# First tokens' pool means taken without the shift and earlier, their row sums later, and two pieces of the scale multiplied on TensorE

## The chip, the cores and the metric

The kernel runs on one core of a Trainium2 chip. The metric is the device time of one execution in microseconds (us); of several runs the median is given.

## The reference

One decoder block over 1024 tokens of width 1024, in float32. A conditioning vector `c` gives six vectors (shift, scale and gate of two halves). What matters here is the first half of the block:

```python
mod = jax.nn.silu(c) @ w_ada + b_ada
shift1, scale1, gate1, shift2, scale2, gate2 = ...
h = rms_norm(x, norm1_pre) * (1.0 + scale1) + shift1
z = h @ w_in                      # 1536 columns: u (512), v (512), pool (512)
y_a = spatial_gating(z[..., : 2 * D_A], ...)
y_b = multiscale_pool(z[..., 2 * D_A:], w_pool, b_pool, pool_scale)
mix = jnp.concatenate([y_a, y_b], axis=-1) @ w_out
x = x + gate1 * rms_norm(mix, norm1_post)
```

The pooling takes, in four groups of 128 channels, the mean over the last 2, 4, 8 or 16 tokens (over fewer at the beginning), subtracts the token itself and multiplies by a 128 by 128 matrix. The second half (a squared-ReLU MLP) is not touched.

## The kernel before

The 1024 tokens are worked in two halves of 512. `start` (L1340 onward) holds the whole first half up to the mixer's output projection, in an order written out by hand for all engines; what follows it up to the MLP (`project` and so on) is put in order by the framework, which may also set some of that work between instructions of `start`. Matrix products are done in three passes of two-part numbers (high part by high part, low by high, high by low), so each weight tile needs a copy on ACT (the high part) and a subtraction on DVE (the low part).

**The scale and the shift.** The rows of `w_ada` for scale 1 come in five pieces (`PIECES`: 128, 128, 256, 256, 256 columns), those for shift 1 in four pieces of 256 columns. `piece_sum` adds the eight rows of a piece on DVE, weighted by `silu_c`, into two running sums (even and odd rows; L1312 and L1314), and `both` (L1318) adds the two. `piece_end` (L1327) multiplies every 128 columns by a column of ones on TensorE, which sums over the partitions, and `ada_vector` (L188, L191) adds bias and gain on DVE. The first two scale pieces are what the first products wait for: `scaled_hi` (L1333, ACT) and `scaled_lo` (L1337, DVE) scale the transposed tokens, and `pool_pass` (L1421) multiplies them with the pool's columns of `w_in`.

**The shift by row sums.** In the first half the tokens are not shifted. The shift's part of `z` is one vector, the weights' rows weighted by the shift and summed. `row_sum` (L1524, L1526) makes that sum on DVE for the pool's columns (`bacc`, from the tiles `braw`), the value columns (`vacc`) and the gate columns (`uacc`), eight steps each; `row_vector` (L1531) sums over the partitions on TensorE. For the pool the vector is added to the four `zbs` by ACT (L1634), and only then `windowed` takes the means (L384 to L399 on DVE): it saves the last 16 tokens in `halo` for the second half, adds the tile to itself shifted one, two or three or four times, corrects the first tokens and subtracts the token.

**The order around it.** After the pool passes come the value products (a loop over four weight tiles, with the shift's pieces on DVE), then the gate passes `gate_pass(0)` to `gate_pass(7)` (L1596), the spatial products (L468), the pool's output (`pool_out`, L417 on TensorE, L419 and L421 on ACT, L422 on DVE), the first weight tiles of the projection (`stream.fill`), and `spatial_end` (L473, L478, then the split at L91 and L94). `load_x(1)` loads the second half's tokens into the four tiles that `braw` lay in, so it waits for the row sums of the pool. `measure` (L308) and `apply` (L317) normalise them.

`project` then multiplies with `w_out` in two passes over columns (L85 to L87, tile `po`); the order of the operands is pool pairs 0 and 1, 2 and 3, then spatial 0 and 1, 2 and 3. Between the two passes it calls `prepare`, which transposes the second half's tokens (L324) and scales them (L329).

```python
MIX_ORDER = (2, 3, 0, 1)
...
            token_pass(ym, MIX_ORDER, f"po{h}_{dh}", done)
            if dh == 0:
                between()
```

Of the kernel before, what the change touches and what calls it, by code (L numbers as in the profile page):

```python
# [8 lines left out]
F32 = mybir.dt.float32  # L9
# [3 lines left out]
ALU = mybir.AluOpType  # L13
# [27 lines left out]
def block_kernel(  # L41
# [1264 lines left out]
    def piece_sum(blk, c0, n, ts):  # L1306

        def step(kt):
            def run():
                acc = acc_of[blk][kt % 2][:, c0:c0 + n]  # L1310
                if kt < 2:
                    nc.vector.tensor_scalar(acc, ts[kt], silu_c[:, kt:kt + 1], None, ALU.mult)  # L1312
                else:
                    nc.vector.scalar_tensor_tensor(acc, ts[kt], silu_c[:, kt:kt + 1], acc, ALU.mult, ALU.add)  # L1314
            return run
        def both():
            a, b = [acc_of[blk][o][:, c0:c0 + n] for o in range(2)]
            nc.vector.tensor_tensor(a, a, b, ALU.add)  # L1318

        return [step(kt) for kt in range(KT)] + [both]  # L1320

    def piece_end(blk, c0, n, split=False):
        pa = ps_tile(f"pa{blk}_{c0}")
        nk = n // P
        for k in range(nk):
            at = c0 + k * P
            nc.tensor.matmul(pa[:, k:k + 1], lhsT=acc_of[blk][0][:, at:at + P], rhs=ones[:, 0:1], start=True, stop=True)  # L1327
        rest = lambda: ada_vector(blk, pa[:, 0:nk], range(c0 // P, c0 // P + nk))
        return rest if split else rest()

# [8 lines left out]
    def start():  # L1339
# [50 lines left out]

        g = piece_sum(1, *PIECES[0], sc[0])
        first(0)
# [9 lines left out]
        third(2)  # L1402
        weave(g)
        second(3)
        scale_rest = piece_end(1, *PIECES[0], split=True)
        third(3)
# [7 lines left out]
        hT = []  # L1414
        pbs = [ps_tile(f"pb0_{j}") for j in range(NG)]

# [16 lines left out]
        hT.append(scaled_hi(pts[0], 0))  # L1433
        g = piece_sum(1, *PIECES[1], sc[1])
        weave(g[:KT // 2])
        scaled_lo(hT[0], pts[0], 0)
        weave(g[KT // 2:])
        pool_lo(0)
        pool_pass(0, 0)
        pool_pass(0, 1)  # L1440
        piece_end(1, *PIECES[1])
        his(1)
        pool_pass(0, 2)
        more(3)
        g = piece_sum(1, *PIECES[2], sc[2])
        weave(g[:KT // 2])
# [58 lines left out]
        value_lo(0, 0)  # L1505
        value_lo(0, 1)
        pool_pass(KT - 1, 1)
        pool_pass(KT - 1, 2)
# [10 lines left out]

        bacc, vacc, uacc = rows_of("b"), rows_of("v"), accp.tile([P, 512], F32, tag="junk", bufs=1, name="shift_wu")  # L1520

# [30 lines left out]
        for kp in range(NQ):  # L1552
            if kp == 0:
                sh.append(piece(0, 2 * QC, QC))
                value_tiles(1)
                value_hi(1)
                gate_load(0)
# [24 lines left out]
            if kp == 1:  # L1582
                rest_b()
                turn()
            if kp == 2:
                offsets()


# [24 lines left out]
        for i in range(NT):  # L1613
            nc.tensor.matmul(pvs[i], lhsT=ones_r, rhs=vb[:, 0], start=False, stop=False)
            nc.tensor.matmul(pvs[i], lhsT=ones_r, rhs=vb[:, 1], start=False, stop=True)
        weave(sums_b(0, 4), sums_u(0, 2))
        gate_load(3)
        gate_pass(2)
        gate_pass(3)
        steps, vs = values(0, pvs)  # L1620
        weave(steps[:4], sums_b(4, 8))
        gate_hi(2)
        gate_lo(2, 0)
        gate_lo(2, 1)
        gate_pass(4)
        weave(steps[4:], sums_u(2, 6))
        gate_hi(3)
        gate_lo(3, 0)
        gate_lo(3, 1)
        gate_pass(5)  # L1630
        bvec = row_vector(bacc, "b")
        for j in range(NG):
            z = zbs[j][:, HALO:]
            nc.scalar.activation(z, z, AF.Identity, bias=bvec[:, j:j + 1])  # L1634
        weave(sums_u(6, 8), windowed(0, 0, zbs[0]))
        gate_pass(6)
# [24 lines left out]
        return ya + [y for y, low in yb]  # L1661


    with tc.manual_schedule(engines={E.DVE, E.Activation, E.PE, E.Pool, E.SP}):
# [45 lines left out]
```

## Time and profile before

| what | value |
|---|---|
| runs | 923.02, 923.35, 924.67 us (median 923.35) |
| profiled execution | 922.04 us, span 920.3 us |
| busy | PE 889.4 us (97%), DVE 687.4 (75%), ACT 419.1 (46%), POOL 89.1 (10%) |
| granted TensorE clock, mean | 0.995 |

Times in the rows are us from the start of the span. PE is TensorE's matmuls, PEld its weight loads, DVE VectorE, ACT ScalarE, POOL GpSimd, SPq the queue from which SyncE issues DMAs. A busy PE in a window is not PE at its peak, since the ends of matmuls are modelled and the next one starts before the last has ended; so the rate of TensorE is better read from the starts of its instructions.

### The profile page before, as it was taken

What the parts mean: (1) busy time and instruction counts of PE and PEld (TensorE: products, weight loads), DVE (VectorE), ACT (ScalarE), POOL (GpSimd) and SP (SyncE); (2) the same over time, 40 slices, a digit from 0 to 9 for tenths busy, and PEclk for the clock granted to TensorE, in tenths of its full rate; (3) what the DMA queues carried; (4) which work ended last, traced back from release to release, by engine and by line L of the source; (5) the groups of instructions that cost most, each with busy time, mean ns of one, the idle gap of its engine ahead of it and who ended that gap; (6) DMA issues with size and microseconds to landing.
All of it is one profiled execution on the core that took longest, in us unless ns stands there. A gap on an engine that the chain in (4) does not pass through costs nothing.

```text
span 920.3 us, 10782 instructions
## 1 busy us (share of the span) xinstructions
PE 889.4 (97%) x3960; PEld 722.9 (79%) x3960; DVE 687.4 (75%) x980; ACT 419.1 (46%) x558; POOL 89.1 (10%) x147
## 2 busy tenths in 40 slices
PE   5999999999999989999999999999999999999995
PEld 3788678888887768888888888778888888888883
DVE  6989888799759896766666657567887774569796
ACT  3323674334367474444444354544455433434331
POOL 4001020013003001111100101100000000000032
PEclk9999999999999999999999999999999999999998
DMA  9934256575734148543444434499975884334664
GB/s 316 357 113 143 91 161 188 178 252 183 234 87 149 54 129 274 185 138 130 168 150 158 139 136 155 160 320 389 338 242 198 294 279 117 109 110 145 207 212 154
DMA packets 114105, 173.52 MB, mean 189 GB/s; under 512 B 6098, under 2 KB 61442, under 8 KB 114052
## 3 DMA queue, kind: packets, MB, share of 16 engines
q1 hardware_dynamic: 104292, 135.03, 45.8%
q0 software_dynamic: 9760, 37.80, 10.8%
q8 instruction: 31, 0.51, 0.2%
q14 instruction: 22, 0.18, 0.1%
HBM read 135.06 MB, written 37.75 MB: 188 GB/s over the span
## 4 chain that ended last, share of the span: by engine, by line
PE 53%; issue 32%; DVE 8%; ACT 4%; DMA 2%; POOL 1%; SPq 0%; POOLq 0%; DVEq 0%; ACTq 0%
PE a L828 6%; PE a L829 6%; PE a L830 6%; PE p L830 3%; PE p L829 3%; PE p L828 3%; PE pb L1421 3%; PE po L85 2%; PE pu L1596 2%; PE po L86 2%; PE po L87 2%; PE pv L85 2%; PE pv L87 2%; PE pv L86 2%; PE b L828 1%
## 5 line engine op out<-in xcount | busy, mean ns | idle before, releaser
L85 PE MATMUL m<-thi,shi 128*128 128x512 f32 x448 | 174.3, 389 | 0.0
L86 PE MATMUL m<-tlo,shi 128*128 128x512 f32 x448 | 174.3, 389 | 0.0
L87 PE MATMUL m<-thi,slo 128*128 128x512 f32 x448 | 174.3, 389 | 0.0
L94 DVE TENSOR_TENSOR slo<-s,shi 128x1024 fp32r<-128x1024 f32 x56 | 68.4, 1222 | 55.8 <-ACT shi L91 55.8
L91 ACT CAST shi<-s 128x1024 fp32r<-128x1024 f32 x56 | 58.9, 1052 | 106.2 <-PE m L86 64.1
L86 PEld LDWEIGHTS m<-tlo,shi 128*128 128x128 f32 x448 | 84.1, 188 | 17.6
L87 PEld LDWEIGHTS m<-thi,slo 128*128 128x128 f32 x448 | 84.1, 188 | 17.5
L85 PEld LDWEIGHTS m<-thi,shi 128*128 128x128 f32 x448 | 84.1, 188 | 17.3
L91 ACT CAST thi<-wt 128x1024 fp32r<-128x1024 f32 x40 | 42.1, 1052 | 39.7 <-DVE wt L571 31.3
L91 ACT CAST whi<-w_raw 128x1024 fp32r<-128x1024 f32 x28 | 29.3, 1053 | 52.0 <-DMA w_raw<-in_w_in_dram 15.4
L571 DVE TENSOR_TENSOR wt<-wt,b 128x1024 f32<-128x1024 f32 x32 | 39.1, 1222 | 15.0 <-DMA b<-in_w_fc_dram 13.1
L94 DVE TENSOR_TENSOR tlo<-wt,thi 128x1024 fp32r<-128x1024 f32 x40 | 48.9, 1223 | 1.4
L571 DVE TENSOR_TENSOR S<-c,F 128x1024 f32<-128x1024 f32 x12 | 14.7, 1224 | 41.8 <-ACT F L860 41.8
L94 DVE TENSOR_TENSOR wlo<-w_raw,whi 128x1024 fp32r<-128x1024 f32 x28 | 34.1, 1220 | 7.0 <-ACT whi L91 7.0
L858 ACT COPY F<-a 128x512 f32<-128x512 f32 x16 | 9.4, 586 | 57.0 <-PE a L830 57.0
L291 POOL TENSOR_TENSOR f<-msf,neg_half 128x1 f32<-128x1 f32 x8 | 7.2, 901 | 282.5 <-DVE msf L1160 282.5
L603 DVE TENSOR_TENSOR lob<-wa,hib 128x1024 fp32r<-128x1024 f32 x16 | 19.6, 1225 | 16.4 <-ACT hib L598 16.4
L598 ACT CAST hic<-wo 128x1024 fp32r<-128x1024 f32 x16 | 16.8, 1051 | 31.3 <-DVE wo L571 31.3
L598 ACT CAST hib<-wa 128x1024 fp32r<-128x1024 f32 x16 | 16.8, 1050 | 30.3 <-DVE wa L571 30.3
L181 DVE SCALAR_TENSOR_TENSOR ada_acc<-ada_raw,silu_c,ada_acc 128x1024 f32<-128x1024 f32 x21 | 26.9, 1280 | 3.9 <-DMA ada_raw<-in_w_ada_dram 3.8
L85 PE MATMUL po<-whi,ybs 128*128 128x512 f32 x64 | 25.8, 406 | 1.6 <-ACT yb L419 0.9
L830 PE MATMUL p<-hS,loc 128*128 128x512 f32 x64 | 25.4, 397 | 1.9 <-DVE loc L603 1.9
(311 smaller groups left out, 2194.4 us busy)
## 6 DMA issues: line engine op xcount, KB each, us to landing
s<-fD SPq DMA_DIRECT2D x56, 512.0 KB, 4.1
wt<-in_w_fc_dram SPq DMA_DIRECT2D x40, 512.0 KB, 5.1
ada_raw<-in_w_ada_dram SPq DMA_DIRECT2D x24, 512.0 KB, 4.8
fD<-S POOLq DMA_DIRECT2D x16, 768.0 KB, 3.7
wa<-in_w_fc_dram SPq DMA_DIRECT2D x20, 512.0 KB, 4.2
piece<-in_w_ada_dram SPq DMA_DIRECT2D x16, 512.0 KB, 8.3
w_raw<-in_w_out_dram SPq DMA_DIRECT2D x16, 512.0 KB, 4.6
wo<-in_w_fc_dram SPq DMA_DIRECT2D x16, 512.0 KB, 4.6
```

Source lines behind the costliest of these rows:

```text
L85: nc.tensor.matmul(ps, lhsT=ah, rhs=bh, start=start, stop=False)
L86: nc.tensor.matmul(ps, lhsT=ah, rhs=bl, start=False, stop=False)
L87: nc.tensor.matmul(ps, lhsT=al, rhs=bh, start=False, stop=stop)
L91: nc.scalar.copy(hi, src)
L94: nc.vector.tensor_tensor(lo, src, hi.bitcast(F32), ALU.subtract)
L181: nc.vector.scalar_tensor_tensor(acc, t, silu_c[:, kt:kt + 1], acc, ALU.mult, ALU.add)
L571: nc.vector.tensor_tensor(o, a, b, op)
L598: nc.scalar.copy(unit_tiles(kind, n)[0], src)
L828: nc.tensor.matmul(ps, lhsT=ah, rhs=bh, start=first, stop=False, skip_group_check=not start)
L829: nc.tensor.matmul(ps, lhsT=ah, rhs=bl, start=False, stop=False, skip_group_check=not start)
L830: nc.tensor.matmul(ps, lhsT=al, rhs=bh, start=False, stop=last, skip_group_check=not start)
L1421: nc.tensor.matmul(pbs[j], lhsT=w[:, j * P:(j + 1) * P], rhs=a, start=k == 0 and n == 0, stop=k == KT - 1 and n == 2)
```

## The change

- The first two pieces of the scale (128 columns each) are no longer summed on DVE. `piece_direct` gives TensorE the eight rows of a piece as stationary operands, with a column of `silu_c` each, and adds them up in PSUM.
- The other seven pieces keep the two running sums on DVE, but `both` is gone: `piece_end` multiplies both sums by ones and adds them in PSUM.
- The pool's row sums are not added to `zbs`. A constant falls out of "mean minus token", so the means of the first half are taken without it, and only the `halo` that the second half reads gets it, in `shift_halo`, called between the two passes of the projection.
- So `windowed(0, 0)` and `(0, 1)` move into the loop of the value products, `(0, 2)` ahead of `gate_pass(2)`; the first three `pool_out` move ahead of `gate_pass(5)`; the first weight tile of the projection is split before `gate_pass(6)`.
- The eight row sums of `bacc` move behind the first two `spatial_end`, and `load_x(1)` and `measure` behind the last.
- The second weight tile of the value products is split before the last pool passes.

```diff
-        def both():
-            a, b = [acc_of[blk][o][:, c0:c0 + n] for o in range(2)]
-            nc.vector.tensor_tensor(a, a, b, ALU.add)
-
-        return [step(kt) for kt in range(KT)] + [both]
+        return [step(kt) for kt in range(KT)]
...
         for k in range(nk):
             at = c0 + k * P
-            nc.tensor.matmul(pa[:, k:k + 1], lhsT=acc_of[blk][0][:, at:at + P], rhs=ones[:, 0:1], start=True, stop=True)
+            for o in range(2):
+                nc.tensor.matmul(pa[:, k:k + 1], lhsT=acc_of[blk][o][:, at:at + P], rhs=ones[:, 0:1], start=o == 0, stop=o == 1)
...
+    def piece_direct(blk, c0, ts):
+        pa = ps_tile(f"pa{blk}_{c0}")
+        for kt in range(KT):
+            nc.tensor.matmul(pa[:, 0:1], lhsT=ts[kt], rhs=silu_c[:, kt:kt + 1], start=kt == 0, stop=kt == KT - 1)
+        return lambda: ada_vector(blk, pa[:, 0:1], range(c0 // P, c0 // P + 1))
...
-        weave(g)
+        scale_rest = piece_direct(1, 0, sc[0])
         second(3)
-        scale_rest = piece_end(1, *PIECES[0], split=True)
         third(3)
         scale_rest()
...
         pool_lo(0)
         pool_pass(0, 0)
+        piece_direct(1, P, sc[1])()
         pool_pass(0, 1)
-        piece_end(1, *PIECES[1])
         his(1)
...
         value_lo(0, 1)
+        value_tiles(1)
+        value_hi(1)
         pool_pass(KT - 1, 1)
...
             if kp == 1:
                 rest_b()
                 turn()
+                weave(windowed(0, 0, zbs[0]))
             if kp == 2:
                 offsets()
+                weave(windowed(0, 1, zbs[1]))
...
-        weave(sums_b(0, 4), sums_u(0, 2))
         gate_load(3)
+        weave(sums_u(0, 2), windowed(0, 2, zbs[2]))
         gate_pass(2)
         gate_pass(3)
         steps, vs = values(0, pvs)
-        weave(steps[:4], sums_b(4, 8))
+        weave(steps[:4])
...
-        weave(steps[4:], sums_u(2, 6))
+        weave(steps[4:], sums_u(2, 4))
...
+        yb = [pool_out(0, j, pair_of(diffs[0], j)) for j in range(3)]
         gate_pass(5)
-        bvec = row_vector(bacc, "b")
-        for j in range(NG):
-            z = zbs[j][:, HALO:]
-            nc.scalar.activation(z, z, AF.Identity, bias=bvec[:, j:j + 1])
-        weave(sums_u(6, 8), windowed(0, 0, zbs[0]))
+        weave(sums_u(4, 6))
+        stream.fill(1)
+        yb[0][1]()
+        yb[1][1]()
         gate_pass(6)
+        weave(sums_u(6, 8))
         gate_pass(7)
         psp = [spatial_products(0, j, vs) for j in range(2)]
         uvec = row_vector(uacc, "u")
         us = [gate(0, j, pus[j], uvec[:, j:j + 1]) for j in range(NHEAD)]
-        weave(windowed(0, 1, zbs[1]), windowed(0, 2, zbs[2]))
         psp += [spatial_products(0, j, vs) for j in range(2, NHEAD)]
-        yb = [pool_out(0, j, pair_of(diffs[0], j)) for j in range(2)]
         weave(windowed(0, 3, zbs[3]))
-        for y, low in yb:
-            low()
-        stream.fill(1)
-        yb += [pool_out(0, j, pair_of(diffs[0], j)) for j in range(2, NG)]
+        yb += [pool_out(0, 3, pair_of(diffs[0], 3))]
+        yb[2][1]()
+        stream.fill(2)
+        yb[3][1]()
+        bacc = accp.tile([P, 512], F32, tag="acc", name="shift_wb")
+        rest_u = sums_b(0, KT)
+        ya = []
+        for j in range(NHEAD):
+            ya.append(spatial_end(0, j, psp[j], us[j]))
+            if j == 1:
+                stream.fill(3)
+            weave(rest_u[4 * j:4 * j + 4])
         load_x(1)
         measure, apply = normalise(1, "a")
-        ya = []
-        for j in range(NHEAD):
-            if j in (1, 2):
-                stream.fill(1 + j)
-            ya.append(spatial_end(0, j, psp[j], us[j]))
-            if j < 2:
-                yb[2 + j][1]()
-            if j == 2:
-                measure()
+        measure()
         apply()
+
+        def shift_halo():
+            bvec = row_vector(bacc, "b")
+            for j in range(NG):
+                nc.vector.tensor_scalar(halo[:, j, :], halo[:, j, :], bvec[:, j:j + 1], None, ALU.add)
+
+        late["halo"] = shift_halo
...
     def prepare(key, h, n, name):
         def run():
+            late["halo"]()
             nxt[key] = hidden(h, n, name)
         return run
```

## Rows read from the trace of the kernel before

**Rows 1.** Windows: stretch, length, busy time (x instructions) of each engine, clock, DMA.

```profile
24.29:46.10 21.81, 21.81 (x107) 17.46 (x107) 20.17 (x48) 8.43 (x15) 0.86 (x5) 1.00 1.07 357
46.10:71.50 25.40, 25.40 (x121) 20.53 (x120) 21.66 (x53) 6.40 (x9) 0.00 (x0) 1.00 0.32 106
71.50:100.50 29.00, 29.00 (x153) 24.81 (x152) 27.31 (x57) 10.69 (x18) 4.14 (x4) 1.00 0.47 145
100.50:107.40 6.90, 5.06 (x13) 1.77 (x12) 6.15 (x10) 6.58 (x11) 0.00 (x0) 1.00 0.00 0
107.40:129.60 22.20, 22.05 (x93) 17.42 (x94) 17.60 (x26) 14.49 (x22) 5.30 (x8) 1.00 0.54 158
```

**Rows 2.** Timeline, 11 to 15 us: start, duration, engine, instruction.

```profile
11.15 0.90 PE L1389 MATMUL pta<-ident,x 128*128 128x128 f32 x3 [0.47 <-DVE x L1385]
13.44 0.58 PE L1327 MATMUL pa<-ones,ada_acc 128*128 128x1 f32 x2 [1.39 <-DVE ada_acc L1318]
14.62 0.69 ACT L1333 ACTIVATE ha<-pta,scale 128x512 fp32r<-128x512 f32 x1 [0.78 <-DVE ada_acc L1312]
```

**Rows 3.** Timeline, 18 to 24.3 us, around the second and third piece.

```profile
18.94 0.42 PE L1327 MATMUL pa<-ones,ada_acc 128*128 128x1 f32 x2
19.22 1.84 PE L1421 MATMUL pb<-ha,wblo 128*128 128x512 f32 x4
20.90 0.60 PE L324 MATMUL pta<-ident,x 128*128 128x128 f32 x4
...
23.34 0.42 DVE L1318 TENSOR_TENSOR ada_acc<-ada_acc,ada_acc 128x256 f32<-128x256 f32 x1
...
23.82 0.61 PE L1327 MATMUL pa<-ones,ada_acc 128*128 128x1 f32 x4 [1.39 <-DVE ada_acc L1318]
```

**Rows 4.** Chain that ended last, around the fourth piece's products: start, length, what.

```profile
30.97 0.34 PE pa L1327 x4
31.31 1.98 PE pb L1421 x8
```

**Rows 5.** Instructions on the sums of the pieces: the additions of both sums.

```profile
L1318 DVE TENSOR_TENSOR ada_acc<-ada_acc,ada_acc x9: 291/424/426, 13.1 to 66.1; 128x256 f32<-128x256 f32 x7, 128x128 f32<-128x128 f32 x2
```

**Rows 6.** Groups of DVE instructions, 92 to 104 us, one addition of the means.

```profile
L389 DVE TENSOR_TENSOR s<-zb 128x527 f32<-128x527 f32 x4 | 2.7, 702 | 0.0
```

**Rows 7.** Chain that ended last, 98 to 101 us.

```profile
98.02 0.79 PE pau L1531 x8
...
100.70 0.88 PE pp L417 x2
```

**Rows 8.** Instructions on zb, 85 to 105 us: ACT's additions of the shift.

```profile
L1634 ACT ACTIVATE zb<-zb,vecb x4: 707/708/723, 90.9 to 92.7; 128x512 f32<-128x512 f32 x4
```

**Rows 9.** Timeline, 104 to 108 us, TensorE's waits ahead of the projection.

```profile
104.26 1.04 ACT L91 CAST whi<-w_raw 128x1024 fp32r<-128x1024 f32 x1
...
107.42 0.50 PE L85 MATMUL po<-whi,ybs 128*128 128x512 f32 x1 [0.88 <-ACT yb L419]
```

**Rows 10.** Instructions on the pool's row sums and on weight splits: ns min/median/max.

```profile
L1526 DVE SCALAR_TENSOR_TENSOR shift_wb<-x,shift,shift_wb x7: 741/745/755, 75.2 to 83.7; 128x512 f32<-128x512 f32 x7
...
L94 DVE TENSOR_TENSOR wlo<-w_raw,whi x7: 1211/1219/1226, 105.3 to 125.9; 128x1024 fp32r<-128x1024 f32 x7
```

**Rows 11.** Timeline, 127 to 130 us, the last spatial end and the second half's tokens.

```profile
127.06 0.68 DVE L94 TENSOR_TENSOR yas<-ya,yas 128x512 fp32r<-128x512 f32 x1
127.66 2.73 DVE L317 TENSOR_SCALAR x<-x,r_a 128x1024 f32<-128x1024 f32 x4
...
129.61 3.65 PE L324 MATMUL pta<-ident,x 128*128 128x128 f32 x32
```

**Rows 12.** Instructions on the second half's token tiles, 70 to 135 us.

```profile
L109 SPq DMA_DIRECT2D x<-in_x_dram x4: 327/328/467, 77.1 to 84.5; - x4
L308 ACT ACTIVATE junka<-x x4: 1054/1057/1058, 119.7 to 123.3; 128x1024 bf16<-128x1024 f32 x4
...
DMA to landing us min/median/max: 4.2/5.0/5.7
```

More of the change, by code (lines that the diff above doesn't have):

```diff
@@ L1315, in step, with piece_end @@
             return run
-        def both():
-            a, b = [acc_of[blk][o][:, c0:c0 + n] for o in range(2)]
-            nc.vector.tensor_tensor(a, a, b, ALU.add)
-        return [step(kt) for kt in range(KT)] + [both]
-    def piece_end(blk, c0, n, split=False):
+        return [step(kt) for kt in range(KT)]
+    def piece_end(blk, c0, n):
         pa = ps_tile(f"pa{blk}_{c0}")
@@ L1326, in piece_end @@
             at = c0 + k * P
-            nc.tensor.matmul(pa[:, k:k + 1], lhsT=acc_of[blk][0][:, at:at + P], rhs=ones[:, 0:1], start=True, stop=True)
-        rest = lambda: ada_vector(blk, pa[:, 0:nk], range(c0 // P, c0 // P + nk))
-        return rest if split else rest()
+            for o in range(2):
+                nc.tensor.matmul(pa[:, k:k + 1], lhsT=acc_of[blk][o][:, at:at + P], rhs=ones[:, 0:1], start=o == 0, stop=o == 1)
+        ada_vector(blk, pa[:, 0:nk], range(c0 // P, c0 // P + nk))
+    def piece_direct(blk, c0, ts):
[3 more added lines that the diff above has]
+        return lambda: ada_vector(blk, pa[:, 0:1], range(c0 // P, c0 // P + 1))
     def scaled_hi(ps, k):
@@ L1389, in third @@
                 nc.tensor.transpose(out=pts[k][:, i * P:(i + 1) * P], in_=xs[i][:, k * P:(k + 1) * P], identity=ident)
-        g = piece_sum(1, *PIECES[0], sc[0])
+        pbs = [ps_tile(f"pb0_{j}") for j in range(NG)]
         first(0)
@@ L1414, in start @@
         hT = []
-        pbs = [ps_tile(f"pb0_{j}") for j in range(NG)]
         def pool_pass(k, n):
@@ L1433, in start @@
         hT.append(scaled_hi(pts[0], 0))
-        g = piece_sum(1, *PIECES[1], sc[1])
-        weave(g[:KT // 2])
+        g = piece_sum(1, *PIECES[2], sc[2])
         scaled_lo(hT[0], pts[0], 0)
-        weave(g[KT // 2:])
         pool_lo(0)
         pool_pass(0, 0)
+        piece_direct(1, P, sc[1])()
         pool_pass(0, 1)
-        piece_end(1, *PIECES[1])
         his(1)
@@ L1444, in start @@
         more(3)
-        g = piece_sum(1, *PIECES[2], sc[2])
         weave(g[:KT // 2])
@@ L1518, in rows_of @@
             return fact.tile([P, 512], F32, tag="f", name=f"shift_w{n}")
-        bacc, vacc, uacc = rows_of("b"), rows_of("v"), accp.tile([P, 512], F32, tag="junk", bufs=1, name="shift_wu")
+        vacc, uacc = rows_of("v"), accp.tile([P, 512], F32, tag="junk", bufs=1, name="shift_wu")
         def row_sum(acc, k, src):
@@ L1554, in start @@
                 sh.append(piece(0, 2 * QC, QC))
-                value_tiles(1)
-                value_hi(1)
                 gate_load(0)
@@ L1640, in start @@
         us = [gate(0, j, pus[j], uvec[:, j:j + 1]) for j in range(NHEAD)]
-        weave(windowed(0, 1, zbs[1]), windowed(0, 2, zbs[2]))
         psp += [spatial_products(0, j, vs) for j in range(2, NHEAD)]
-        yb = [pool_out(0, j, pair_of(diffs[0], j)) for j in range(2)]
         weave(windowed(0, 3, zbs[3]))
-        for y, low in yb:
-            low()
-        stream.fill(1)
-        yb += [pool_out(0, j, pair_of(diffs[0], j)) for j in range(2, NG)]
+        yb += [pool_out(0, 3, pair_of(diffs[0], 3))]
[10 more added lines that the diff above has]
+            weave(rest_u[4 * j:4 * j + 4])
         load_x(1)
         measure, apply = normalise(1, "a")
-        ya = []
-        for j in range(NHEAD):
-            if j in (1, 2):
-                stream.fill(1 + j)
-            ya.append(spatial_end(0, j, psp[j], us[j]))
-            if j < 2:
-                yb[2 + j][1]()
-            if j == 2:
-                measure()
-        apply()
+        measure()
+        apply()
+        def shift_halo():
[3 more added lines that the diff above has]
+        late["halo"] = shift_halo
         return ya + [y for y, low in yb]
+    late = {}
     with tc.manual_schedule(engines={E.DVE, E.Activation, E.PE, E.Pool, E.SP}):
```

## The prediction

> **What bounds the kernel now.** I read the windows first, then the chain, then the timelines of the two places where TensorE stands still. In the windows from 24.29 to 100.50 us TensorE's busy time equals the length of each stretch, while DVE has 1.6 to 3.7 us left in each [rows 1]; the chain runs through TensorE there, piece by piece without a gap [rows 4]. So each instruction added to TensorE in that stretch is paid in full, and each freed on DVE or ACT is worth something only through what it lets start earlier. Two places are open. At the start, up to 24 us, the products wait for the scale: TensorE waits 1.39 us for the first piece's sum and again 1.39 us for the third's [rows 2, 3]. And ahead of the projection, in 100.50 to 107.40 us, TensorE has 13 instructions only [rows 1]. From 107.42 us on the projection runs steadily [rows 9], and behind it TensorE stays the bound, since its busy share of the whole span is 97%; what is won or lost by 133 us should reach the end unchanged.
>
> **The start.** The first piece loses about 2.3 us of sums on DVE and gains eight products on TensorE, 16 instructions, since such a float32 product is two (two instructions for the one product of the second piece [rows 3]). Behind a full queue two of them take 0.28 us, 18.94 to 19.22 [rows 3], thus 0.14 each and 2.24 us a piece. The bounds are 0.085 (a quarter of the 0.34 of four at TensorE's other speed [rows 4]) and 0.29 (half of the 0.58 from a standstill [rows 2]). I take 0.14, because the eight follow each other and TensorE is as slow there. The transposes of the third tile end at about 11.9, so the products end at 14.1 and the scaling, 0.6 us behind the old ones' end at 14.02 [rows 2], starts at about 14.85 in place of 14.62. The second piece's products go behind the first pass (four matmuls, 1.75 us from 15.6), 17.35 to 19.6, against an end at 19.22 before [rows 3]: 0.4 us later. From there DVE's chain to the third piece's products is the same, less `both` (0.42 us [rows 3]), plus four products (0.34 us [rows 4]): a gain of 0.08. So the start is **+0.3 us**, with bounds of -1.6 (0.085 each, both pieces) and +3.0 (0.29 each, the second piece partly hidden). DVE's saved sums are worth nothing here: the wait moves from DVE to TensorE.
>
> **TensorE's clock.** The pool pass at 19.22 us takes 1.84 us for four matmuls, about 0.44 each, though the row grants 1.00; from 31.31 eight take 1.98, 0.25 each [rows 3, 4]. That is the lower level, 1.2 GHz, and then 2.4 GHz; it rose at about 20.9 us, where four transposes go in 0.35 us [rows 3], behind the first tile's pool passes. The Trainium skill (TensorE: Matmul & The Clock Gate, "What's actually happening") says that the slow state is the default and that activity releases it. By that rule the direct products, which fill the gap before 13.44, could bring the rise forward; it is a rival below, priced from the rows.
>
> **The other pieces.** Seven `piece_end` get four more instructions each; the third piece's are in the sum above, six remain: 6 x 0.34 = **+2.04 us** [rows 4], all on TensorE where nothing covers it. The lower bound is 0, if their weight loads hid under the matmuls in front; but the old four did not. A rule speaks against the change here: the Trainium skill (TensorE: Matmul & The Clock Gate, "LDWEIGHTS (loading the stationary operand)") puts a load at columns divided by 1.2 per ns, 107 ns for 128 columns. By it the six pieces would cost 2.6 us; the row's 0.085 us is shorter, and the row decides.
>
> **DVE in the loop of the value products.** Each `both` of 256 columns frees 0.42 us [rows 5]: four in this loop, 1.7. `windowed(0, 0)` and `(0, 1)` bring three additions and two subtractions of 0.70 [rows 6], 3.5 us, and four short ones on 16 columns; I count 4.2 us. From 21.66 of 25.40 us [rows 1] DVE goes to 24.2 of 26.8 (four pieces at 0.34 longer). I cost this at nothing: the cover is 2.6 us, and the shift's pieces are needed one weight tile later. The earlier copy of the second weight tile gives DVE another 2 us at the loop's beginning.
>
> **The pool's vector.** Its eight products, 0.79 us like the gate's [rows 7], leave the gate stage: **-0.79 us**. ACT's four additions of 0.71 [rows 8] leave too; ACT is half idle there [rows 1], so that is worth nothing by itself.
>
> **The idle time ahead of the projection.** From the spatial products' end at 100.70 [rows 7] to 107.42 [rows 9] are 6.72 us. In it lie eight pool products' instructions of 0.44 (0.88 for two [rows 7]), 3.5 us, and three matmuls of the projection, 0.7. So 2.57 us are idle. With three of the four pool products, the first weight tile and two operands ready earlier, the projection can start right behind the fourth: **-2.57 us**; the bound on the other side is 0.
>
> Up to there: 0.3 + 2.04 - 0.79 - 2.57 = -1.0 us.
>
> **The projection's first pass.** What is late next is DVE. In 107.40 to 129.60 us it has 4.6 us left [rows 1], and eight row sums come in: 8 x 0.745 = 6.0 us by duration [rows 10], about 5.3 by their starts. They stand between the spatial ends, ahead of the third weight tile's low part (1.22 us [rows 10]) and of the last two operands. Also the second weight tile's high part now stands on ACT behind the gates and the fourth pool output, where DVE waits for it, as ACT's copy stood at 104.26 before [rows 9]. The last operand was ready at 127.74 [rows 11] and TensorE's last matmuls just behind it, so it cannot come later without moving the pass's end. My count has DVE reach it between 127 and 129, so the pass ends at about 129.6 as before, and the 1.0 us that TensorE had won is lost again: **+1.0 us**, between 0 and +2. Then the pool's products come back, **+0.79 us**, between 0 (hidden in TensorE's wait) and 0.79.
>
> **Sum.** -1.0 + 1.0 + 0.8 = +0.8 us on 922.04 of the profiled execution, 922.8; the median of the runs lies 1.31 above that execution, so I forecast 924.2. A measurement of this kernel can tell about 0.2%, 1.85 us.
>
> **The rivals.**
> - *The second half's tokens are late (slower).* `load_x(1)` went out from 77.1 to 84.5 and was squared by 119.7 to 123.3, 1.2 us a tile [rows 12]. Now the last tile is free only after the row sums, at about 121.9; 4.2 to 5.0 us to landing [rows 12] make 126.5. ACT squares behind the last spatial end, four times 1.2 from about 126.4: 131.1; the power on POOL and the scaling bring 132.8. The transposes started at 129.61 [rows 11]; if they keep their place and wait for the last tile, they end 2.9 us later. It decides as soon as the tokens are scaled later than about 130.5 and the framework has set no products of the second pass in front. For it: the move behind all spatial ends. Against: the framework orders this part and may fill it. In place of the 0.8: 0.4 + 2.9 = +3.3, **926.7**.
> - *All of TensorE's win is kept*, because DVE's waits for ACT are filled with splits and the last operand comes in time: -1.0 + 0.8 = -0.2, **923.1**. For it: the splits of later tiles already stand between spatial ends. Against: 6.0 us into 4.6.
> - *The clock rises early*, at or before 17 us. The second piece's products take 0.085 and the passes 0.23 each, so the third piece comes 1.5 to 2 us sooner: **922.2**, or 921.2 with the rival before. Against: between 12 and 15 us the engine still stands.
> - *The clock stays low longer or the direct products cost 0.29*: +2.5 more, **926.7**.
> - *The change does not close the gap*: TensorE still waits for ACT ahead of the projection, as it did for 0.88 us on the pool output [rows 9], since the fourth output and the second tile stay late. Then the 2.57 stay: **926.8**.
>
> **How the numbers follow.** The forecast gets 0.40, late tokens 0.24, the kept win 0.12, the early clock 0.16, the late one 0.04, the open gap 0.04. Faster by over 0.2% (below 921.5) is most of the early clock and a part of the kept win: 0.18. Slower (above 925.2) is the late tokens, the two last cases and the edge of the forecast: 0.35. The rest, 0.47, is no change. The range reaches from the early clock with the kept win, 921.0, to late tokens with some of the start's upper bound, 927.4. The forecast's own is 922.8 to 925.4, from 0 to +2 in the pass and the start's smaller errors.
>
> **What would show it.** Right: 16 instructions on the first piece in about 2.2 us; eight in 0.68 for each later piece; no wait ahead of the projection; the row sums between spatial ends, and TensorE waiting there for a split or a spatial operand. Wrong: transposes that wait for the scaled tokens (the first rival), a matmul of 0.23 us before 19 us (the clock), a wait of the gate passes on DVE (my cover in the loop), or a first pass that ends before 129 us.

## The result and the profile after

The changed kernel takes 939.55 us (937.38 to 939.84, 4 runs), the kernel before 923.79 beside it (923.02 to 924.67): a ratio of 1.0165, with a 95% interval of [1.0147, 1.0184], 15.8 us slower. The forecast was 924.2, at most 927.4. The profiled execution is the fastest of the four (the others take 939.4 to 939.8): 937.38 us, its span 935.3; that is 15.0 us over the span before, and the difference is whole by the second pass of the projection: the transposes ahead of it end at 148.65 us where they ended at 133.26 [rows 11], 15.4 later.

**Where it builds up.** First TensorE's timeline at the start, which answers [rows 2, 3]. L1331 is a direct piece, L1324 the third piece's products, L1423 the pool's passes.

```profile
12.38 3.41 PE L1331 MATMUL pa<-silu_c,piece 128*128 128x1 f32 x16
...
18.89 3.41 PE L1331 MATMUL pa<-silu_c,piece 128*128 128x1 f32 x16
22.16 2.05 PE L1423 MATMUL pb<-ha,wbhi 128*128 128x512 f32 x4
24.01 1.91 PE L1423 MATMUL pb<-ha,wblo 128*128 128x512 f32 x4
...
26.43 1.46 PE L1423 MATMUL pb<-ha,wbhi 128*128 128x512 f32 x4
27.72 0.95 PE L1324 MATMUL pa<-ones,ada_acc 128*128 128x1 f32 x8
28.53 1.18 PE L1423 MATMUL pb<-ha,wbhi 128*128 128x512 f32 x4
```

The next work starts 3.27 us after a direct piece's first instruction: 0.20 us for each of the 16, not 0.14. And the passes at 22.16 and 24.01 take 0.43 to 0.46 us a matmul, the lower level of 1.2 GHz; only the pass at 26.43 gets faster. Before, that happened at 20.9 us [rows 3]. The third piece's products end at 28.53 instead of 24.29: **+4.2**. About half a us of that is the tokens' arrival, which differs between executions: the last transposes ahead of the first piece's products start at 11.69 us, where they started at 11.15 [rows 2].

The windows behind it, in the columns of [rows 1]: stretch, length, busy time of PE, PEld, DVE, ACT and POOL, granted clock.

```profile
28.53:78.14 49.61, 49.61 (x250) 40.86 (x250) 42.74 (x103) 14.37 (x22) 0.83 (x5) 1.00 0.54 181
78.14:109.30 31.16, 31.16 (x154) 25.30 (x152) 24.91 (x48) 13.87 (x21) 3.37 (x4) 1.00 0.29 86
109.30:143.48 34.18, 26.42 (x106) 19.70 (x104) 24.56 (x39) 16.56 (x27) 3.09 (x4) 0.94 0.59 184
143.48:148.65 5.17, 5.17 (x33) 5.17 (x34) 4.93 (x7) 4.34 (x12) 4.95 (x5) 0.71 0.19 32
```

From the third piece's products to the gate the kernel before needed 47.21 us, 24.29 to 71.50 [rows 1]; now it is 49.61, without idle time: **+2.4**, six pieces with four more instructions each, 0.40 a piece. A later piece in the chain, eight instructions where [rows 4] had four in 0.34:

```profile
35.25 0.78 PE pa L1324 x8
36.03 1.98 PE pb L1423 x8
```

Then comes what the change was for: TensorE is busy in all 31.16 us up to the projection.

```profile
108.84 1.02 PE L417 MATMUL pp<-diff,wpl 128*128 128x512 f32 x2
109.30 0.80 PE L85 MATMUL po<-whi,ybs 128*128 128x512 f32 x1
```

The projection begins right behind the last pool product, without the waits of [rows 9]. Counted by the steady pace of 0.23 us a matmul, it began before at 107.42 less the three matmuls already done, 106.7, and now at 109.7 (its second matmul starts at 109.93), 3.0 later. Start and pieces had put it 6.6 late: the gap and the pool's vector gave back **3.6**.

And the pass that follows loses that and much more: 33.8 us to the first transpose instead of 22.9, **+10.9**, and another 1.5 in the transposes. TensorE is busy for 26.42 of 34.18 us. Its waits there, us in total, times, longest:

```profile
PE pta L324 <- DVE x L317: 2.7, 1, 2.7
PE po L85 <- ACT yas L91: 2.0, 1, 2.0
PE po L85 <- ACT whi L91: 1.7, 1, 1.7
PE pab L1532 <- DVE shift_wb L1527: 1.1, 1, 1.1
```

They are 7.5 us. The rest is the pool vector's products, now here, and slow matmuls: behind the wait for the third spatial operand one starts only every 0.43 us, and the 32 transposes take 5.17 us in place of 3.65 [rows 11], at a granted clock of 0.71. An estimate of what the slow instructions add: seven matmuls from 133.19 take 3.1 us where 0.23 each make 1.6, and with the 1.5 of the transposes that is about 3 us.

```profile
133.19 0.80 PE L85 MATMUL po<-whi,yas 128*128 128x512 f32 x1 [2.05 <-ACT yas L91]
133.78 0.63 PE L86 MATMUL po<-wlo,yas 128*128 128x512 f32 x1
134.21 0.63 PE L85 MATMUL po<-whi,yas 128*128 128x512 f32 x1
...
143.48 5.17 PE L324 MATMUL pta<-ident,x 128*128 128x128 f32 x32 [2.71 <-DVE x L317]
```

The order in time is waits first, clock second: up to 130 us the row grants 1.00, though the wait for the third weight tile (1.72 us, ending at 122.77) and the one for the row sums (1.14) lie there, and only behind them it falls.

```profile
120.00:130.00 10.00, 7.17 (x29) 4.87 (x27) 9.03 (x12) 5.43 (x6) 0.00 (x0) 1.00 0.67 190
130.00:140.00 10.00, 7.78 (x30) 6.08 (x31) 7.55 (x15) 4.21 (x10) 0.95 (x1) 0.83 0.75 270
```

Who is late is read from the timelines of DVE and ACT: four row sums hold the second spatial end; the second operand's cast at 121.15 waits 4.91 us for it; and the third weight tile's cast, with which TensorE starts at 122.77, stands behind that cast.

```profile
116.88 0.48 DVE L1525 TENSOR_SCALAR shift_wb<-x,shift 128x512 f32<-128x512 f32 x1
117.40 2.33 DVE L1527 SCALAR_TENSOR_TENSOR shift_wb<-x,shift,shift_wb 128x512 f32<-128x512 f32 x3
...
137.48 0.75 DVE L179 TENSOR_SCALAR ada_acc<-ada_raw,silu_c 128x1024 f32<-128x1024 f32 x1 [2.24 <-DMA ada_raw<-in_w_ada_dram]
138.15 0.69 DVE L94 TENSOR_TENSOR yas<-ya,yas 128x512 fp32r<-128x512 f32 x1
...
142.69 2.73 DVE L317 TENSOR_SCALAR x<-x,r_a 128x1024 f32<-128x1024 f32 x4
```
```profile
121.15 0.62 ACT L91 CAST yas<-ya 128x512 fp32r<-128x512 f32 x1 [4.91 <-DVE ya L478]
121.67 3.90 ACT L91 CAST whi<-w_raw 128x1024 fp32r<-128x1024 f32 x4
```

Later DVE waits 2.24 us for a transfer of the gate vector's weights (L179), with the last operand's low part behind it in its queue; and the tokens, loaded from 118.2 to 130.1 instead of 77.1 to 84.5 [rows 12], are scaled at 142.69.

### The profile page after: what moved, and what is told of

Same layout as the page of the kernel before. It is cut to its first block, busy times and chain, and to the rows that moved or that the text cites. A ratio compares the mean times of both kernels' runs of the same rounds, so it can differ in the third digit from the quotient of the medians.

```text
span 935.3 us, 10873 instructions
## 1 busy us (share of the span) xinstructions
PE 900.9 (96%) x4016; PEld 735.5 (79%) x4016; DVE 681.3 (73%) x959; ACT 417.1 (45%) x554; POOL 90.3 (10%) x147
## 3 DMA queue, kind: packets, MB, share of 16 engines
q0 software_dynamic: 9760, 37.80, 10.5%
## 4 chain that ended last, share of the span: by engine, by line
PE 54%; issue 31%; DVE 8%; ACT 3%; DMA 2%; POOL 1%; SPq 0%; POOLq 0%; DVEq 0%; ACTq 0%
PE a L828 5%; PE a L829 5%; PE a L830 5%; PE pb L1423 3%; PE p L830 3%; PE p L829 3%; PE p L828 3%; PE po L87 2%; PE pu L1597 2%; PE po L85 2%; PE po L86 2%; PE pv L85 2%; PE pv L87 2%; PE pv L86 2%; PE b L828 1%
## 5 line engine op out<-in xcount | busy, mean ns | idle before, releaser
L85 PE MATMUL po<-whi,yas 128*128 128x512 f32 x64 | 25.8, 411 | 3.8 <-ACT yas L91 2.0
```

Of the source, the lines that this page charges most:

```text
L85: nc.tensor.matmul(ps, lhsT=ah, rhs=bh, start=start, stop=False)
```

## The experiments

All on the same kernel size, each beside runs of the kernel before (923.1 to 923.9 in the five sets; each difference is to its own set). **My theory after the result:** three independent losses, the one-column products on TensorE at the start, the doubled products of six pieces, and an order of the projection's first pass that makes DVE, ACT and the queues wait in turn. **The rivals:** the parts act on each other; or the low clock is the cause and the waits follow from it; or DVE simply has too much work in the pass.

### The three parts alone

The kernel before with the two direct pieces alone (`piece_direct` for the first two `piece_sum`, `both` kept for the others):

> The kernel before with only the first two scale pieces multiplied directly on TensorE. Theory (each part costs by itself): the 16 instructions of a piece take 3.2 us at the lower clock, as in the changed kernel, the second piece's stand between two pool passes, and the clock rises later; the value products then begin about 4 us later and the time is 927 to 929 us. Rival (the loss lies in the tail alone and the start's delay is taken up later, where the engines wait for each other anyway): within 1 us of before.

927.09, ratio 1.0045 [1.0028, 1.0062]: **+4.0**.

The kernel before with the doubled products alone, in the seven pieces of 256 columns:

```diff
-        return [step(kt) for kt in range(KT)] + [both]
+        return [step(kt) for kt in range(KT)] + ([both] if n == P else [])
...
-            nc.tensor.matmul(pa[:, k:k + 1], lhsT=acc_of[blk][0][:, at:at + P], rhs=ones[:, 0:1], start=True, stop=True)
+            for o in range(1 if n == P else 2):
+                nc.tensor.matmul(pa[:, k:k + 1], lhsT=acc_of[blk][o][:, at:at + P], rhs=ones[:, 0:1], start=o == 0, stop=o == 1 or n == P)
```

> The kernel before with only the seven pieces of 256 columns changed: no addition of the two sums on DVE, twice the products on TensorE. Theory: eight instructions take 0.79 us in place of 0.34 for four, seven times 0.45 us, of which the third scale piece gets 0.4 back since DVE's addition ahead of it is gone: 2.5 to 3.1 us slower, 926 to 926.5. Rival (the loads hide behind the matmuls): no change, with 0.34 us of pace lost in no piece.

925.78, ratio 1.003 [1.0018, 1.0042]: **+2.7**.

The rest of the change alone: scale and shift summed as before, with pool means, halo, row sums and token loads of the changed kernel.

> The kernel before with the scale and the shift as they were, and everything else of the change: means early, pool outputs early, the pool's row sums behind the first two spatial ends, tokens loaded and measured last. Theory: the idle 2.6 us ahead of the projection go, and behind it the row sums cost about 8 us of waits (third weight tile, third and fourth spatial operand, tokens) and 2 to 3 us of lower clock after them: 930 to 932 us, with waits of TensorE at the same places as in the changed kernel. Rival (the tail suffers only because TensorE's work before it has become longer, and the clock fell by itself): 921 to 925.

933.02, ratio 1.011 [1.0095, 1.0125]: **+9.9**. Its list of waits has the same four entries as the changed kernel's, with the same durations. 4.0 + 2.7 + 9.9 = 16.6, and the whole change is 15.8 in its own set. Within what such differences can tell (each is known to 1 to 2 us) the parts add, so the first rival falls, and they can be looked at one by one. The second falls with the order in time: here too the first three waits stand in stretches at a granted clock of 0.98 to 1.00 (115 to 128 us), and the row reads 0.50 only from 128 to 131.

### The start

The first direct piece alone:

> The kernel before with the first piece alone by direct products; the second piece summed on the vector engine as before. Both direct pieces together gave 927.09 against 923.1, +4.0. Theory (each piece puts its own 3.2 us of one-column products on TensorE's path): about half, +1.5 to +2.5. Rival 1 (the first is covered by TensorE's own waits for tokens and the second alone costs): within 0.6 of before. Rival 2 (the first delays the rise of the granted clock and carries nearly all): +3 to +4.

924.14 against 923.58, ratio 1.0008 [0.9999, 1.0017]. The first rival was right: the first piece costs 0.6 us, which is not clear of noise, so by the medians the second carries about 3.4 of the 4.0. Below, the timelines with the first piece alone and with both, from the first pool pass to the next transposes:

```profile
16.57 3.18 PE L1426 MATMUL pb<-ha,wbhi 128*128 128x512 f32 x8 [0.48 <-ACT ha L1340]
19.59 0.28 PE L1327 MATMUL pa<-ones,ada_acc 128*128 128x1 f32 x2
19.73 1.17 PE L1426 MATMUL pb<-ha,wblo 128*128 128x512 f32 x4
20.74 0.60 PE L324 MATMUL pta<-ident,x 128*128 128x128 f32 x4
```
```profile
17.42 2.08 PE L1426 MATMUL pb<-ha,wbhi 128*128 128x512 f32 x4 [0.48 <-ACT ha L1340]
19.29 3.41 PE L1335 MATMUL pa<-silu_c,piece 128*128 128x1 f32 x16
22.56 2.05 PE L1426 MATMUL pb<-ha,wbhi 128*128 128x512 f32 x4
24.41 1.91 PE L1426 MATMUL pb<-ha,wblo 128*128 128x512 f32 x4
26.12 0.84 PE L324 MATMUL pta<-ident,x 128*128 128x128 f32 x4
```

4.17 us there and 8.70 here. With eight matmuls of 512 columns in a row the speed changes among them (3.18 us for eight, then 1.17 for four); with one-column products between the fourth and the fifth, the eight that follow are all slow. In all four traces with the second direct piece (those of the changed kernel and of three runs) the passes get fast only at 26.4 to 26.7 us, in all others by about 22. So the second piece costs its own 3.3 us and some 1.4 of slow passes behind it (twelve matmuls of the pool in 5.4 us instead of 4.0). Of that, 1.5 us would have been lost anyway, since the first of the two kernels then waits 1.54 us for the third piece's sum and the other does not.

How the 4.0 is shared is known to about 1 us only. With the first piece alone the passes behind that wait are slow again (1.91 us for four at 25.87; the granted clock reads 0.72 from 24 to 28 us). So its gate passes begin at 73.2 us and those with both pieces at 75.0, only 1.8 apart; in the kernel before they began at 71.5 [rows 1]. Five of the twelve traces with the old start show this second slow stretch too; in one of them, the control below, it puts the gate passes at 72.6.

The clock was my next suspect: 34 instructions of idle products of `ones` from 1 us on, ahead of and among the first work, with both direct pieces.

> The kernel of the run with the direct pieces alone, with 17 idle products of ones added on TensorE from 1 us on, so that it is at work before the first tokens come. Theory (the lower clock sets the price of a direct piece): if the clock is up by 12 us the 16 instructions take 1.6 us in place of 3.2 and the passes 0.23 us a matmul, and the time falls from 927.1 to 922 to 924. Rival (0.2 us is the price of a load from a fresh tile at any clock, or the clock does not rise on such products): 926 to 928.

926.66 (924.8 to 927.0), ratio 1.0028 [1.0016, 1.004]: +2.8 in its own set against +4.0 without them, with intervals that overlap, and a miss of the 922 to 924 of my theory. Its windows, and its idle products:

```profile
5.00:10.00 5.00, 3.45 (x20) 2.72 (x19) 1.78 (x8) 3.39 (x7) 1.79 (x3) 0.98 0.99 325
10.00:15.00 5.00, 4.53 (x21) 4.24 (x21) 1.98 (x4) 1.68 (x4) 4.66 (x8) 0.50 1.13 338
15.00:20.00 5.00, 4.52 (x18) 3.73 (x17) 1.66 (x4) 0.69 (x1) 1.97 (x4) 0.50 1.09 358
...
27.00:29.00 2.00, 2.00 (x12) 1.72 (x11) 1.13 (x5) 0.31 (x1) 0.00 (x0) 1.00 1.06 371
```
```profile
1.11 5.46 PE L1402 MATMUL idle<-ones 128*128 128x128 f32 x24 [1.11 <-DVE ones L122]
...
7.44 1.16 PE L1402 MATMUL idle<-ones 128*128 128x128 f32 x8
```

They went from 0.23 us an instruction to 0.145, so the upper level was reached; but TensorE waited 0.33 and 0.98 us for tokens at 8.9 and 10.5, and the granted clock was back at 0.50 from 10 us on, before the first direct piece. What a direct piece costs at the upper level was therefore not seen.

### The projection's first pass

Row sums ahead of the second weight tile, in the changed kernel:

```diff
+        bacc = accp.tile([P, 512], F32, tag="acc", name="shift_wb")
+        weave(sums_b(0, KT))
+        load_x(1)
         stream.fill(2)
...
-            weave(rest_u[4 * j:4 * j + 4])
-        load_x(1)
+            if j == 2:
+                measure()
```

> The changed kernel, with one thing moved: the eight row sums of the pool and the loading of the second half's tokens stand ahead of the second weight tile, where DVE waits 4.2 us for ACT, and the tokens are measured behind the third spatial end as before. Theory: the waits behind the projection's begin go and the clock does not fall there: 8 to 9 us faster than the changed kernel, 930 to 932. Rival (the tail's loss is the clock or the order that the framework makes, not the row sums): 936 to 940.

942.05, worse than the changed kernel: a miss that says how the queues are tied. I had put the token loads ahead of the weight tile as well. They wait for the row sums, the tile's load stands behind them on SP's queue, ACT's cast behind that, and TensorE waits 6.7 us for it:

```profile
121.03 1.04 ACT L91 CAST whi<-w_raw 128x1024 fp32r<-128x1024 f32 x1 [9.71 <-DMA w_raw<-in_w_out_dram]
```

The same on the tail alone, with the token loads behind the third weight tile's (`load_x(1)` after `stream.fill(3)`, at the second spatial end) and the squares of the tokens (`measure`) behind the third spatial end, where the kernel before has them:

> The kernel of the run with the tail alone, with the eight row sums moved ahead of the second weight tile's low part (where DVE waits 4.2 us for ACT), the tokens' loads behind the third weight tile's load this time, and the tokens measured behind the third spatial end. Theory (the row sums between the spatial ends make the tail's loss): the waits for the third tile, the third spatial operand and the tokens shrink to 1 or 2 us together, the clock stays up, 921 to 925 us. Rival (what costs is the number of jobs on DVE behind the projection's start, wherever the sums stand): 929 or more.

927.16, ratio 1.0041 [1.0026, 1.0056]: +3.3 in its own set, so **6.6 us** of the tail's 9.9 are back, for the three moves together; it falls between my theory (up to 925) and the rival (929 or more). The waits for the third weight tile, for the row sums and for the tokens are gone; one is left, 4.9 us for the last spatial operand. On DVE the gate vector's first step stands between that operand's two halves and waits for its transfer:

```profile
126.73 0.75 DVE L179 TENSOR_SCALAR ada_acc<-ada_raw,silu_c 128x1024 f32<-128x1024 f32 x1 [1.25 <-DMA ada_raw<-in_w_ada_dram]
127.40 0.68 DVE L478 TENSOR_TENSOR ya<-ya,u 128x512 f32<-128x512 f32 x1
128.16 1.29 DVE L181 SCALAR_TENSOR_TENSOR ada_acc<-ada_raw,silu_c,ada_acc 128x1024 f32<-128x1024 f32 x1
129.36 0.69 DVE L94 TENSOR_TENSOR yas<-ya,yas 128x512 fp32r<-128x512 f32 x1
```

So I moved that vector's tiles two weight tiles later in the stream, once in this kernel and once, as a control, in the kernel before:

```diff
-    spread(2, 8, 2, 2)
+    spread(2, 10, 2, 2)
```

> The tail with its row sums early (927.16 against 923.87), and now the eight row tiles of the gate vector's sum two weight tiles later in the stream, so that on the vector engine its first step stands behind the last spatial operand instead of between that operand's two halves. Theory (what is left of the tail's loss is the vector engine's wait for that transfer, 1.25 us at 126.73 plus the 0.75 and 1.29 us of the two steps themselves, which hold the last spatial operand until 130.05 while TensorE stands idle for 4.9 of the ten microseconds from 120): the transposes begin at about 130 instead of 133.85, and the time is 922.5 to 924.5. Rival (the granted clock, 0.82 and 0.84 in 120 to 140, falls for another reason and the transposes stay late): 926.5 to 928.

> The kernel before with only those eight row tiles two weight tiles later: the control of the run beside it. In the kernel before the first step of this sum stands behind all four spatial operands and the four scalings of the tokens, and nothing waits for it there. Theory: no change, 923 to 924.8. Rival (the vector is then late for the second half, or its transfers collide with other tiles): 925 or more.

924.97 (923.7 to 926.3), ratio 1.0018 [1.001, 1.0027], and the control 923.37, ratio 1.0 [0.9991, 1.0009]: +1.4 in place of +3.3, another **1.9 us** back, and worth nothing where the order was good. The 1.4 us were left although the projection began 2.7 us sooner than before (104.0 against 106.7, counted as above). In the profiled execution (925.89) TensorE waited 3.0 us for the last operand, which stands behind the four squares of the tokens. One kernel put the squares one spatial end earlier, one behind the last:

> The tail with its row sums early and the gate vector's sum later (924.97 against 923.58), and now the four token squares issued one spatial end earlier: the tokens are loaded by about 112, and the scalar engine has idle stretches of 4.99 and 2.15 us from 106 to 114, while it squares at 120.15 to 125.65. In that run TensorE waits 3.01 us at 127.93 for the last spatial operand, which stands on the vector engine behind the fourth square. Theory (the order alone of squares and last operand holds the pass): the last operand comes 2 to 3 us sooner, the transposes begin at 129.5 to 130.5 instead of 132.2, and the time is 922 to 923.5. Rival (the vector engine is full in this stage, and what it does sooner holds something else, the third spatial operand or a weight tile's split): 924.3 to 926.

> The same kernel with the squares behind the last spatial end, as the change has them, instead of earlier. The last spatial operand is then held by no square. Theory: TensorE's wait of 3.01 us for that operand shrinks to under 1 us, but the squares (four of 1.25 us on the scalar engine) start at about 124.5, so the scaled tokens come after 130 and the transposes wait for them instead, by 1 to 3 us: 924 to 926, no gain over 924.97, with the wait moved from the operand to the tokens. Rival (the operand's wait alone counted): 922 to 923.5.

926.98, ratio 1.0036 [1.0023, 1.0048]: the squares between the weight casts hold both last operands, and TensorE's wait is 4.3 us. My theory missed; what the rival named came true, that something else is held, but by squares on ACT and not by a full DVE, and the time is above its 924.3 to 926 too. Behind the last end 923.91, ratio 1.001 [1.0001, 1.0019], a little below my 924 to 926: the operand's wait is gone and TensorE waits for the tokens.

```profile
PE pta L324 <- DVE x L317: 2.8, 1, 2.8
```

With none ahead the tokens are late, with four the operand. So one or two of them go into ACT's idle stretch at 119.4 and the others behind (`measure` takes a range of tiles for it):

```diff
+            if j == 2:
+                measure(0, 2)
...
-        measure()
+        measure(2)
         apply()
```

> The kernel with the squares behind the last spatial end gave 923.91 against 923.57: TensorE there has finished the pass early and waits 2.8 us for the scaled tokens. Here one of the four squares goes ahead of the last weight tile's split, where the scalar engine is idle for 1.96 us (119.40 to 121.36 in that run); the three others stay behind. Theory (the order alone is left, a stage with all its work in idle stretches keeps the early start): the wait of 2.8 us shrinks by about 1.25 and the last operand is not later, 922 to 923.2, below the kernel before. Rival (the vector engine or the scalar engine is full, what is won is lost elsewhere): 923.5 to 925.

> The same with two squares ahead of that split, 2.5 us of them in an idle stretch of 1.96, so the split comes 0.5 us later. Theory: the tokens come 2.5 us sooner, the last operand 0.5 to 1.5 us later, and the pass waits 1 to 2 us for the one or the other: 921.5 to 923. Rival (the last operand behind two squares holds the pass as it did behind four): 923.5 to 925.

One: 923.09, ratio 0.9997 [0.9988, 1.0005]. Two: **921.62**, ratio 0.9976 [0.9967, 0.9985], faster than both kernels, though I had still expected a wait of 1 to 2 us. Its list of waits of TensorE from 95 to 150 us is empty, the window from 120 is full at a granted clock of 1.00, and its transposes start at 127.17 instead of 129.61 [rows 11].

```profile
120.00:130.00 10.00, 9.95 (x56) 7.87 (x55) 8.36 (x18) 9.27 (x21) 5.04 (x8) 1.00 0.73 208
```
```profile
127.17 2.09 PE L325 MATMUL pta<-ident,x 128*128 128x128 f32 x16
```

DVE and ACT do the same work in it as in the run of +9.9 us (busy 690.5 and 416.4 us of the span, there 688.6 and 416.8). So the rival that DVE has too much work falls; the order alone is worth 12 us by differences to their own sets (9.9 + 2.1).

### Single moves on the kernel before

The token loads and squares behind all spatial ends, nothing else:

> The kernel before with only this moved: the second half's tokens are loaded and measured behind the last spatial end; the row sums stay early. Theory: the squares start on ACT behind the last operand at 126.6 us in place of 119.7, so the transposes wait 2 to 3 us: 925 to 926.5. Rival (the framework sets work of the second pass in front of the transposes, or the loads hide): within 1 us of before.

927.77 (924.9 to 928.7), ratio 1.004 [1.0028, 1.0052]: +3.9. The profiled execution, 924.98, is one of the two shortest of eight, and TensorE waits 2.4 us there for the scaled tokens. The mechanism of my first rival thus exists alone, and that wait is near the 2.9 that I gave it. Why the other six take 927.5 or more is open, since none of them has a profile.

The means early and without the shift, with row sums and token loads in their old places:

> The kernel before with its scale, shift, row sums and token loads where they were, and of the change only the means without the shift, the first two means in the loop of the value products, two pool outputs ahead of the sixth gate pass and two weight tiles split early; the pool's vector goes to the halo between the two passes. Theory (closing the gap is right, the late sums are the fault): the idle 2.6 us ahead of the projection go and nothing comes in their place, 920 to 921.5 us. Rival (DVE becomes the bound of the value products or of the projection's first pass when the means move): 923 or more.

924.27, ratio 1.0002 [0.9993, 1.0011]; the rival was right. The gap does not close, since DVE is full: busy 51.22 us of the 54 from 52 to 106, with the row sums still among the gate passes.

```profile
PE pp L417 <- DVE diff L399: 2.3, 1, 2.3
PE pu L1598 <- DVE wuwlo L1551: 1.0, 1, 1.0
```

Only the first weight tile's split earlier (`stream.fill(1)` ahead of `gate_pass(6)`):

> The kernel before with only the split of the projection's first weight tile moved ahead of the seventh gate pass; pool means, row sums, halo and token loads as before. Theory (before the projection TensorE waits for this split, which stands behind the first two pool vectors on the scalar engine, 104.26 plus 1.04, and on the vector engine 105.33 plus 1.23, while the scalar engine is idle from 93.4 to 98.8): the projection begins at 104.1 to 105 instead of 106.5, and the time is 921.5 to 923, faster than both kernels. Rival 1 (the 1.23 us on the vector engine, now within its chain of window sums, which has no idle time between 93 and 104, hold the pool vectors as much as is won): 923.3 to 924.3. Rival 2 (the projection's first pass gives it back, waiting for its third spatial operand and the tokens' scales): 923.3 to 924.3, with a start of the projection that is early.

924.77, ratio 1.0017 [1.0008, 1.0026]: not faster, and the first rival's mechanism. The split's low part, 1.22 us at 95.92, enters DVE's chain of means, and TensorE waits for the last mean instead of the split:

```profile
105.89 1.10 PE L417 MATMUL pp<-diff,wpl 128*128 128x512 f32 x2 [1.47 <-DVE diff L399]
```

It waits another 1.8 us for the last spatial operand, for which the kernel before has no wait. In the tail alone, where the row sums have left the gate stage, the gap is closed. So it is the sums that have to go, and then to be put where nothing waits behind them.

## Why the prediction was wrong

- **The projection's first pass** is the step that failed: +1.0, "between 0 and +2". I set six us of row sums against 4.6 us that DVE had left, let the last operand come in time all the same, and so counted as cost only that TensorE's earlier 1.0 us would be lost. In the tail alone the forecast's terms (-0.79 - 2.57 + 1.0 + 0.79) make -1.6; it measured +9.9. Not DVE's sum of work failed but the order: row sums between the spatial ends hold ACT's casts, which hold DVE's low parts; the tokens' loads wait for the row sums, and a transfer that DVE waits for came to stand between an operand's halves. Runs showed 6.6 us for the sums moved ahead together with the token loads and squares, 1.9 for the transfer, and 3.5 for the place of the four squares (from +1.4 to -2.1). In a good order the tail measured -2.1, beyond the -1.6, with the same work. The clock falls in the pass too, behind the first waits, and that is about 3 us of the changed kernel's trace by the estimate above. No run has these four waits without the slow stretch, so the two were not separated; in the last version both are gone, and the row reads 1.00.
- **The start**, +0.3 with bounds of -1.6 and +3.0, was mis-sized, beyond its upper bound: +4.2 in the trace, +4.0 for the two pieces alone. I took 0.14 us an instruction from a row where two were issued, 16 took 0.20. And I took the clock's rise at 20.9 as given and gave a late one a chance of 0.04: behind the direct products it came at 26. The rival of an early rise (0.16), for which I had drawn on the Trainium skill (TensorE: Matmul & The Clock Gate, "What's actually happening"), went the other way. By that rule the added products could bring the rise forward; the traces agree that the slow state comes first, and the rise came later with them.
- **The other pieces**: +2.04, measured +2.4 in the trace, 0.40 a piece. For the seven alone 2.7. Mechanism right, and nothing covered them, as forecast. An estimate from the figure of the Trainium skill (TensorE: Matmul & The Clock Gate, "LDWEIGHTS (loading the stationary operand)", 107 ns for 128 columns) would have given 2.6: in this run closer than my 0.085 us from one row.
- **DVE in the loop of the value products** cost nothing, as forecast: no wait of TensorE from 28.6 to 110 us.
- **The gap and the pool's vector**: -2.57 and -0.79, together -3.4, measured -3.6. Right.
- **Late tokens**, the first rival: its mechanism is there, 2.7 us of wait against 2.9, but behind an operand that is itself late, so that the rival's 926.7 fell far short. No case of mine had several of these waits at once; the forecast and its rivals each took one at most.

## What to carry to other kernels

When work moves into a stage where two engines hand parts back and forth, free time of the engine is no price: write the queues of all engines down in their new order, loads too, and look for what stands behind each instruction that waits. A gain that opens a gap earlier is only kept if every later due date moves with it; here the same work in another order was worth 12 us of 923. And sums by one-column products are cheap to write and dear to run on an engine that is the bound.

## What I had not expected of the hardware

- Sixteen instructions of one column take 3.3 us at the start, 0.20 each, against 0.10 later (0.78 us for eight): about the factor between the matmuls of 512 columns at the two levels (0.46 and 0.25).
- The granted clock of the page reads 1.00 in the first 26 us of the kernel with both direct pieces and 0.50 with the idle products added, for the same passes of 2.05 us. With the first piece alone, the row reads 1.00 before the rise and 0.72 in the second slow stretch. At the start the durations tell the level, and in these three traces the row did so only where the level had been up before.
- Two waits of 0.33 and 0.98 us, with three short transposes between them, were followed by a granted clock of 0.50 until about 26 us, though 16 idle products had come before.
